# Two running sums of a depthwise convolution: from SBUF tiles to two PSUM banks

## The chip, the core and the metric

The kernel runs on one core of one Trainium2 chip. The metric is device time in microseconds (us) of one execution; lower is better. Five engines work side by side, each through its own queue in order: TensorE (PE, matmuls, with its weight loads as PEld), VectorE (DVE), ScalarE (ACT), GpSimd (POOL) and SyncE (SP, which here only issues DMAs). SBUF is the on-chip memory for operands, PSUM the memory of eight banks into which PE writes.

## What is computed

A trunk of four layers over 512 image tokens and 256 context tokens of width 1024: attention, neighbourhood attention, a convolution module, a Fourier mixer, each followed by an MLP of width 4096. The change is in the third mixer, which works on the image tokens alone:

```python
def conv_module(h, w_pw1, b_pw1, w_dw, b_dw, ln_g, ln_b, w_pw2, b_pw2):
    a, g = jnp.split(h @ w_pw1 + b_pw1, 2, axis=-1)
    u = a * jax.nn.sigmoid(g)
    pad = CONV_WIDTH // 2            # CONV_WIDTH = 31
    u = lax.conv_general_dilated(u, w_dw[:, None, :], window_strides=(1,), padding=[(pad, pad)],
                                 dimension_numbers=('NWC', 'WIO', 'NWC'),
                                 feature_group_count=u.shape[-1]) + b_dw
    u = jax.nn.silu(layer_norm(u, ln_g, ln_b))
    return u @ w_pw2 + b_pw2
```

For each feature the convolution is a sum of 31 products: tap t of that feature times the token sequence moved by t.

## The kernel before

Features lie on partitions, 128 at a time, so the 1024 features are eight blocks j = 0 to 7, each a tile of 128 partitions by 512 tokens. Matmuls take their operands as two parts (high and low, made by `split`, lines 101 to 104), and `mm3` (lines 119 to 126) makes three matmuls of each product: lines 123, 124 and 126.

The convolution layer is `l2` (line 909). Its main loop runs over the eight blocks. For a block it loads and splits two weight tiles (ACT makes the high part `wh`, POOL the low part `wl` for j > 0), lets PE make the two halves of the first projection in `ps_mm` (48 matmuls), and calls `conv_input` (line 1087 on): ACT takes the sigmoid (L1091), DVE makes `u` from PSUM (L1095), ACT rounds it to `uH` (L1100), DVE makes the rest `uL` (L1102). Then the taps of the block follow, in `conv_taps` (line 1104), for blocks 0 to 6:

- The first 9 taps (10 in blocks 5 and 6, `PE_TAPS`) go to PE as diagonal matrices `dg`, which ACT makes in pairs (L1112, L1113, four buffers each); their sum, with a mean that is taken off (L1116), comes about in `ps_cv`.
- The other 22 (21) taps are DVE's. `acc` holds two sums, `y` and a temporary `tmp_t`, both in SBUF. The first two taps start the sums (L1122, L1124); each further one is a scalar_tensor_tensor, acc = u * w + acc, alternating between the sums (L1126, 138 in all). Then DVE adds the two sums (L1128) and PE's part (L1130).

The finished `y` is summed up with its square for the layer norm: ACT squares it (L943), POOL adds both (L941, L944). Block 7 has no taps on DVE: ACT and POOL make all its 31 diagonals beforehand (L953, L954, five after each block), and PE makes its taps for half the tokens at a time (L960, L963, L964). Behind the first half and 36 matmuls of the second stands the column sum of the statistics (L981), which needs all sums, and with it the layer norm of the first half of the tokens begins.

Order: DVE's instructions in this stage are kept in program order (`keep`), as are the diagonals of block 7. `advance` interleaves them: the taps of block j - 1 on DVE run while PE makes the projection of block j, and `u` of block j stands among them. All else is ordered by a scheduler that simulates the program. PSUM in this layer has four banks for `mm`, two for `cv` and two for `st`; `st` is used by the statistics before and behind the taps, and by nothing during them.

Of the kernel before, what the change touches and what calls it, by code (L numbers as in the profile page):

```python
# [10 lines left out]
R = mybir.dt.float32r  # L11
# [5 lines left out]
P = 128  # L17
# [10 lines left out]
TAPS = 31  # L28
# [5 lines left out]
# columns of the vector table  # L34
# [14 lines left out]
class Trunk:  # L49
# [10 lines left out]
    # ---------------------------------------------------------------- pools  # L60
# [14 lines left out]
    def psum(self, pool="psum", **roles):  # L75
        """PSUM tiles by role: name = (banks of a tile, tiles)."""
        if pool in self.pools:
            self.close(pool)
        p = self.open(pool, space=bass.MemoryType.PSUM)
        for r, (banks, bufs) in roles.items():  # L80
            self.roles[r] = p, banks, bufs
# [14 lines left out]
    # ---------------------------------------------------------------- pieces  # L96
    def load(self, dst, src):
        """a load that none traced later overtakes"""
        self.last_load = self.tc.keep_in_program_order(self.nc.sync.dma_start(dst, src)).ins

    def split(self, src, H, L, low=None):
        """H + L = src, both with float32r's 12 significant bits."""
# [3 lines left out]
    def weight(self, src, pool=None, n=P, bufs=None, raw_bufs=None, low=None):  # L106
        """A block of 1024 rows and n columns, split: [P, KC, n] twice."""
# [11 lines left out]
    def mm3(self, outs, lhs, rhs, k, last):  # L119
        """outs[i] += (lH + lL)^T (rH + rL), without the product of the two low parts."""  # L120
# [7 lines left out]
    def rstd(self, ss, n, role="n"):  # L128
        """(ss / n + eps) ** -0.5, with a Newton step behind the square root's table"""
# [11 lines left out]
    def bcast(self, cols, nb):  # L141
        """[tokens, 1] columns -> every partition holds all tokens (in PSUM)."""
# [15 lines left out]
    def part(self, t, c0, c1):  # L158
        """a part of the tokens: c0:c1, or the image rows that make up c0:c1 of the natural order"""
# [4 lines left out]
    def like(self, t):  # L164
        """a compact tile of such a part"""
# [5 lines left out]
    def modulate(self, j, c0, c1, Rp, gs, sh, hj):  # L171
        """hj <- split(x_j * R * g * (1 + scale) + shift)"""
# [8 lines left out]
    def stat(self, j, c0, c1, S, add=None):  # L181
        """S += x_j^2"""
# [25 lines left out]
    # ---------------------------------------------------------------- ada_ln  # L208
# [15 lines left out]
    def ada_dots(self, t, vs, cols):  # L224
        """The second of two vectors goes to GpSimd and ScalarE, in place."""
# [12 lines left out]
    def ada_finish(self, layer, g, vs):  # L238
        """Bias of chunk group g, and the products that the norms and the biased layers want."""
# [34 lines left out]
    def load_sb(self, nv):  # L274
        """silu of the conditioning vectors, in every partition."""
# [4 lines left out]
    # ---------------------------------------------------------------- phases  # L280
# [25 lines left out]
    def mod_tile(self, l, nv):  # L306
        """The six modulation vectors of layer l as columns, and the products made of them."""
# [10 lines left out]
    def start(self):  # L318
# [8 lines left out]
        # silu of the conditioning vectors, as columns and in every partition  # L327
# [22 lines left out]
        # modulation, norm and the products for k and v advance together over the features  # L350
# [30 lines left out]
        def shift(i):  # L381
            """the shift of half the features, as rows, then as columns"""
# [35 lines left out]
    # ------------------------------------------------------ layer 0: attention  # L418
# [41 lines left out]
    def qk_unit(self, ps, tp, a, g, wk, tab, qkg):  # L460
        """rms norm, rope, split and transpose of 256 tokens x 4 heads (a: 0 q, 1 k)."""
# [58 lines left out]
    def recip_rows(self, sums, w, wk, rp):  # L520
        """1 / sums [P queries, blocks, 2 heads] -> rows [(head, feature), query]"""
# [12 lines left out]
    def fold(self, pv, hh, t):  # L534
        """t's rows of head hh <- the sum of the products with V's high and low parts"""
# [4 lines left out]
    def scale_pv(self, t, rb, dst):  # L540
        """dst <- split(t * rb)"""
# [4 lines left out]
    def l0b(self):  # L546
# [11 lines left out]
        # 256 latent queries, then 256 more, then the context's own, which see the context only  # L558
# [6 lines left out]
        def front(pair, part, hh, u):  # L565
            """the probabilities of 128 queries, transposed and split"""
# [26 lines left out]
        def back(pair, part, hh, half):  # L593
            """half of the keys: both parts of V, side by side, against the split probabilities"""
# [31 lines left out]
        # output projection  # L626
# [17 lines left out]
    # ---------------------------------------------------------------- linear  # L644
    def proj_part(self, wtiles, acts, c0, c1, md, gate, gs, sh, md_next, h_next, rate=0, role="mm", early=0):
        """x += gate * (W^T acts) for the tokens c0:c1, then their norm into h_next."""
# [26 lines left out]
    def mlp(self, layer, T, next_h):  # L673
        """next_h(): opens the tiles that the norm after this block fills."""
# [60 lines left out]
    def swap_h(self, T, name):  # L735
        """Replaces the dead tiles of h by new ones on the same side."""
# [6 lines left out]
    # -------------------------------------------- layer 1: neighbourhood attention  # L743
    def l1a(self):
        """q, k, v of all heads, split, into scratch memory."""
# [7 lines left out]
        # bias and mask of a head: zeros for the context, then the three cases of the window  # L753
# [13 lines left out]
        # v keys: context chunks, then latent chunks that start 8 columns before a block  # L767
# [41 lines left out]
    def l1b(self):  # L809
# [29 lines left out]
        def front(head, b):  # L839
            """the probabilities of 128 queries, transposed and split"""  # L840
# [18 lines left out]
        def back(head, part):  # L859
            """a quarter of a head's products with v"""  # L860
# [6 lines left out]
            # context chunks serve all queries; latent chunk j serves the blocks j - 1 and j  # L867
            for vc in ((0,), (1,), (3, 4), (5, 2))[part]:
                for s in range(2):
# [6 lines left out]
                    elif j > 0:  # L876
                        # second half of the window of block j - 1, first half of that of block j
# [33 lines left out]
    # -------------------------------------------- layer 2: convolution module  # L911
    def l2(self):
# [9 lines left out]
        # the mean of the first 128 features is taken off all of them before the statistics  # L922
# [23 lines left out]
        # all taps of the last features go to the tensor engine, for half of the tokens at a time  # L946
# [375 lines left out]
```

## Time and profile before

| | |
|---|---|
| timed runs | 2802.20, 2808.11 and 2809.17 us, median 2808.11 |
| span of the profiled execution | 2802.3 us; no other time of it is listed, and the fastest timed run is 0.1 us shorter |
| busy over the span | PE 95%, DVE 66%, ACT 42%, POOL 16% |
| stage of the taps on DVE | from 1743 to 1904 us of the span |

The busy shares are means over the whole trunk, in which stages with different limits follow each other. How long an engine was busy in a stage, and what it or the next engine waited for, is read in the stage's own window. An instruction's duration can overlap the next one's start on the same engine, so the pace of a row of instructions is the difference of their starts.

### The profile page before, as it was taken

To read this page: it belongs to the slowest core of one execution; us is meant where nothing else is said; L and a number is where in the kernel's file an instruction comes from. 1 tells how busy PE (TensorE), PEld (TensorE's weight loads), DVE (VectorE), ACT (ScalarE), POOL (GpSimd) and SP (SyncE) were. 2 spreads that over 40 slices of the span, in tenths; PEclk is the share of its full clock that TensorE was granted. 3 is DMA by queue.
4 is the path that set the end of the run, shared out by engine and by line. 5 is a ranking of instruction groups with operands and counts; after the bars stand their busy time and mean duration, and the time that the engine had idled before them with its cause. 6 is when DMAs were issued, how large, how long until landed. Compare 5 with 4: busy or idle time off the path is not lost.

```text
span 2802.3 us, 39962 instructions
## 1 busy us (share of the span) xinstructions
PE 2648.6 (95%) x15452; PEld 2329.9 (83%) x15452; DVE 1841.1 (66%) x2868; ACT 1169.6 (42%) x2087; POOL 460.6 (16%) x373
## 2 busy tenths in 40 slices
PE   5978989999999999999999999888999998999998
PEld 3967878888888888988988889668888887988888
DVE  8897989766453372268766657998766657744435
ACT  4438884312121352278522336444422335533323
POOL 4251122000000040034200005452100003200002
PEclk9989999999999999999999999989999999999999
DMA  7251135344443257488466634112466643333334
GB/s 265 66 169 38 35 125 188 107 149 140 151 139 98 68 161 215 135 202 209 153 207 206 200 117 142 46 53 68 142 200 201 202 127 128 122 105 98 95 95 126
DMA packets 124557, 384.86 MB, mean 137 GB/s; under 512 B 17232, under 2 KB 37840, under 8 KB 123088
## 3 DMA queue, kind: packets, MB, share of 16 engines
q1 hardware_dynamic: 121104, 379.16, 43.5%
q10 hardware_dynamic: 3264, 3.15, 0.3%
q8 instruction: 122, 2.00, 0.3%
q14 instruction: 67, 0.55, 0.1%
HBM read 354.98 MB, written 27.26 MB: 136 GB/s over the span
## 4 chain that ended last, share of the span: by engine, by line
PE 45%; DVE 8%; ACT 1%; DMA 1%; issue 1%; POOL 1%; DVEq 0%; ACTq 0%; POOLq 0%; SPq 0%
PE ps_mm L123 14%; PE ps_mm L126 14%; PE ps_mm L124 14%; DVE y L1126 2%; DVE tmp_t L1126 2%; DMA k<-k 1%; DVE wl L104 1%; DVE h L179 0%; PE ps_s L846 0%; PE ps_pt L855 0%; PE ps_cv L960 0%; PE ps_cv L963 0%; DVE cv L1042 0%; PE ps_cv L964 0%; DVE u L1095 0%
## 5 line engine op out<-in xcount | busy, mean ns | idle before, releaser
L103 ACT CAST wh<-raw 128x1024 fp32r<-128x1024 f32 (+1 forms) x397 | 419.6, 1060 | 1030.6 <-PE ps_mm L124 609.4
L104 DVE TENSOR_TENSOR wl<-raw,wh 128x1024 fp32r<-128x1024 f32 (+1 forms) x368 | 464.8, 1265 | 372.9 <-ACT wh L103 370.1
L191 POOL TENSOR_TENSOR S<-S,tmp_q 128x256 f32<-128x256 f32 (+1 forms) x104 | 145.4, 1398 | 1680.1 <-ACT tmp_q L190 1677.7
L123 PE MATMUL ps_mm<-u,wh 128*128 128x512 f32 (+1 forms) x1088 | 374.9, 346 | 0.0
L124 PE MATMUL ps_mm<-u,wh 128*128 128x512 f32 (+1 forms) x1088 | 373.8, 345 | 0.0
L126 PE MATMUL ps_mm<-u,wl 128*128 128x512 f32 (+1 forms) x1088 | 373.6, 346 | 0.0
L124 PE MATMUL ps_mm<-hm,wh 128*128 128x512 f32 (+1 forms) x912 | 331.0, 365 | 0.0
L126 PE MATMUL ps_mm<-hm,wl 128*128 128x512 f32 (+1 forms) x912 | 330.8, 365 | 0.0
L123 PE MATMUL ps_mm<-hm,wh 128*128 128x512 f32 (+1 forms) x912 | 328.1, 366 | 1.5 <-ACT hm L178 1.1
L203 DVE SCALAR_TENSOR_TENSOR x<-ps_mm,mod,x 128x256 f32<-128x256 f32 (+1 forms) x192 | 114.8, 602 | 247.3 <-PE ps_mm L126 247.3
L220 DVE CUSTOM_DVE_ANT_0 prod<-araw,sb 128x1024 bf16<-128x1024 f32 x216 | 272.7, 1262 | 1.4 <-DMA araw<-in_ada 0.5
L124 PEld LDWEIGHTS ps_mm<-u,wh 128*128 128x128 f32 x1088 | 206.1, 189 | 25.1
L123 PEld LDWEIGHTS ps_mm<-u,wh 128*128 128x128 f32 x1088 | 205.7, 189 | 25.4 <-DVE x L203 0.4
L126 PEld LDWEIGHTS ps_mm<-u,wl 128*128 128x128 f32 x1088 | 205.8, 189 | 25.0
L126 PEld LDWEIGHTS ps_mm<-hm,wl 128*128 128x128 f32 x912 | 172.4, 189 | 27.5 <-DVE wl L104 0.4
L124 PEld LDWEIGHTS ps_mm<-hm,wh 128*128 128x128 f32 x912 | 172.5, 189 | 27.3
L123 PEld LDWEIGHTS ps_mm<-hm,wh 128*128 128x128 f32 x912 | 170.7, 190 | 29.2 <-ACT hm L178 1.5
L103 ACT CAST u<-tmp_r 128x512 fp32r<-128x512 f32 (+2 forms) x143 | 89.1, 624 | 170.7 <-DVE tmp_r L703 170.5
L123 PE MATMUL ps_big<-hm,wh 128*128 128x512 f32 x464 | 157.4, 339 | 0.8 <-ACT wh L103 0.8
L104 DVE TENSOR_TENSOR u<-tmp_r,u 128x512 fp32r<-128x512 f32 (+2 forms) x143 | 99.0, 695 | 86.5 <-ACT u L103 86.2
L124 PE MATMUL ps_big<-hm,wh 128*128 128x512 f32 x464 | 145.9, 337 | 0.0
L123 PE MATMUL ps_mm<-wh,h 128*128 128x256 f32 x448 | 131.3, 294 | 10.2 <-ACT h L178 6.6
(317 smaller groups left out, 5956.1 us busy)
## 6 DMA issues: line engine op xcount, KB each, us to landing
raw<-in_w SPq DMA_DIRECT2D x288, 512.0 KB, 3.9
araw<-in_ada SPq DMA_DIRECT2D x176, 512.0 KB, 3.7
raw<-in_wo SPq DMA_DIRECT2D x32, 512.0 KB, 4.0
raw<-in_wpw SPq DMA_DIRECT2D x24, 512.0 KB, 3.6
raw<-in_wqk SPq DMA_DIRECT2D x16, 512.0 KB, 4.1
q<-q SPq DMA_DIRECT2D x32, 256.0 KB, 8.1
raw<-in_wft SPq DMA_DIRECT2D x16, 512.0 KB, 3.8
k<-k SPq DMA_DIRECT2D x32, 224.0 KB, 8.4
```

The lines of the kernel that those rows point to most:

```text
L103: self.nc.scalar.copy(out=H, in_=src)
L104: (low or self.nc.vector).tensor_tensor(out=L, in0=src, in1=H.bitcast(F), op=ALU.subtract)
L123: mm(o, lhs[0], rh, start=(k == 0), stop=False)
L124: mm(o, lhs[0], rl, start=False, stop=False)
L126: mm(o, lhs[1], rh, start=False, stop=last)
L191: (add or nc.gpsimd).tensor_tensor(out=S[:, :w], in0=S[:, :w], in1=q, op=ALU.add)
L203: self.nc.vector.scalar_tensor_tensor(out=xm, in0=self.like(ps), scalar=gate[:, m:m + 1], in1=xm, op0=ALU.mult, op1=ALU.add)
L220: ins = self.nc.vector.tensor_tensor_reduce(out=junk, in0=t, in1=self.sb[:, v], op0=ALU.mult, op1=ALU.add, scale=1.0, scalar=0.0, accum_ou ...
L1126: keep(nc.vector.scalar_tensor_tensor(out=a, in0=ut, scalar=wt, in1=a, op0=ALU.mult, op1=ALU.add))
```

## The change

`acc` becomes two PSUM tiles of the role `st` in place of `y` and `tmp_t`. The last tap of the first sum writes `y` in SBUF, and the addition of the two sums takes its first input from PSUM. The number of instructions on every engine stays.

```diff
-        acc = (y, self.tmp("t"))
+        acc = [self.ps("st") for _ in range(2)]
...
             else:
-                keep(nc.vector.scalar_tensor_tensor(out=a, in0=ut, scalar=wt, in1=a, op0=ALU.mult, op1=ALU.add))
+                last = t >= TAPS - 2 and a is acc[0]
+                keep(nc.vector.scalar_tensor_tensor(out=y if last else a, in0=ut, scalar=wt, in1=a, op0=ALU.mult, op1=ALU.add))
             yield
-        keep(nc.vector.tensor_tensor(out=y, in0=y, in1=acc[1], op=ALU.add))
+        keep(nc.vector.tensor_tensor(out=y, in0=acc[1], in1=y, op=ALU.add))
```

(The full diff also drops comments, which moves line numbers by one: L1126, L1128 and L1130 of before are L1127, L1129 and L1131 now.)

DVE, from the last taps of block 0 to the first of block 1, before (the names ahead of the arrow are written, those behind it read; the numbers on `y` tell the tiles of blocks apart):

```order
L1126 SCALAR_TENSOR_TENSOR y_16663<-u,vecs,y_16663 128x512
L1126 SCALAR_TENSOR_TENSOR tmp_t<-u,vecs,tmp_t 128x512
L1128 TENSOR_TENSOR y_16663<-y_16663,tmp_t 128x512
L1130 TENSOR_TENSOR y_16663<-ps_cv,y_16663 128x512
L1122 TENSOR_SCALAR y_16664<-u,vecs 128x512
L1124 TENSOR_SCALAR tmp_t<-u,vecs 128x512
L1126 SCALAR_TENSOR_TENSOR y_16664<-u,vecs,y_16664 128x512
```

Here each tap reads two tiles in SBUF, `u` and the sum (`vecs` holds the tap's weight, one number for each partition), and writes SBUF. The same place on DVE in the changed kernel:

```order
L1127 SCALAR_TENSOR_TENSOR y_16663<-u,vecs,ps_st 128x512
L1127 SCALAR_TENSOR_TENSOR ps_st<-u,vecs,ps_st 128x512
L1129 TENSOR_TENSOR y_16663<-ps_st,y_16663 128x512
L1131 TENSOR_TENSOR y_16663<-ps_cv,y_16663 128x512
L1122 TENSOR_SCALAR ps_st<-u,vecs 128x512
L1124 TENSOR_SCALAR ps_st<-u,vecs 128x512
L1127 SCALAR_TENSOR_TENSOR ps_st<-u,vecs,ps_st 128x512 x10
```

Nothing moved on DVE; the sums did, so that each of these reads one tile in SBUF at most, and all but three of a block write PSUM.

The scheduler's order of the other engines shifts a little with it. ACT around the square of block 2's `y` (L943), before (`dg` are PE's diagonals of the next taps, `wh` a weight tile's high part, `tmp_q` the sigmoid):

```order
L943 ACTIVATE tmp_r<-y_16665 128x512
L953 ACTIVATE dg_16673<-ident,wdH 128x128 x5
L103 CAST wh<-raw 128x1024
L1091 ACTIVATE tmp_q<-ps_mm,vecs 128x512
L1112 ACTIVATE dg_17424<-ident,wdH 128x128
L1113 ACTIVATE dg_17425<-ident,wdL 128x128
```

And in the changed kernel:

```order
L103 CAST wh<-raw 128x1024
L1091 ACTIVATE tmp_q<-ps_mm,vecs 128x512
L1112 ACTIVATE dg_17427<-ident,wdH 128x128
L1113 ACTIVATE dg_17428<-ident,wdL 128x128
L1112 ACTIVATE dg_17434<-ident,wdH 128x128
L1113 ACTIVATE dg_17435<-ident,wdL 128x128
L943 ACTIVATE tmp_r<-y_16665 128x512
```

The weight tile, the sigmoid and two pairs of diagonals moved ahead of the square, which waits for DVE's L1131. The order in which PE mixes taps and projection shifts by a few matmuls in the same way, and POOL takes some weight tiles before a sum instead of behind it.

## Rows read from the trace of the kernel before

**Rows 1.** Chain of waits, 1743 to 1904 us: shares by engine, tile, line.

```profile
by line: DVE y L1126 34.2%; DVE tmp_t L1126 27.1%; DVE tmp_t L1124 4.1%; DVE u L1095 3.8%; DVE y L1128 3.5%; DVE y L1130 2.6%; DVE uL L1102 2.5%; DVE y L1122 2.5%; PE ps_cv L960 2.5%; PE ps_cv L963 2.4%; PE ps_cv L964 2.3%; issue 1.7%; POOL
```

**Rows 2.** Windows, block 2: length, PE, PEld, DVE, ACT, POOL, clock, DMA, GB/s.

```profile
1812.00:1836.00 24.00, 19.13 (x72) 15.19 (x71) 23.86 (x27) 11.54 (x30) 12.55 (x11) 0.86 0.21 66
```

**Rows 3.** Waits, 1743 to 1903 us: total us, times, longest.

```profile
ACT uH L1100 <- DVE u L1095: 37.2, 6, 8.6
...
PE ps_cv L123 <- ACT dg L1112: 17.2, 6, 4.9
```

**Rows 4.** Timeline of DVE and POOL: start us, duration us, instruction.

```profile
1769.50 0.74 DVE L1126 SCALAR_TENSOR_TENSOR tmp_t<-u,vecs,tmp_t 128x512 f32<-128x512 f32 x1
1769.90 2.62 POOL L104 TENSOR_TENSOR wl<-raw,wh 128x1024 fp32r<-128x1024 f32 x1 [4.40 <-ACT wh L103]
1770.16 2.90 DVE L1126 SCALAR_TENSOR_TENSOR y<-u,vecs,y 128x512 f32<-128x512 f32 x1
1772.98 0.74 DVE L1126 SCALAR_TENSOR_TENSOR tmp_t<-u,vecs,tmp_t 128x512 f32<-128x512 f32 x1
```

**Rows 5.** DVE's groups, 1743 to 1904 us: count, busy us, mean ns, idle before.

```profile
L1126 DVE SCALAR_TENSOR_TENSOR y<-u,vecs,y 128x512 f32<-128x512 f32 x70 | 73.1, 1044 | 0.0
L1126 DVE SCALAR_TENSOR_TENSOR tmp_t<-u,vecs,tmp_t 128x512 f32<-128x512 f32 x68 | 59.1, 869 | 0.0
L1128 DVE TENSOR_TENSOR y<-y,tmp_t 128x512 f32<-128x512 f32 x7 | 9.0, 1287 | 0.2
L1124 DVE TENSOR_SCALAR tmp_t<-u,vecs 128x512 f32<-128x512 f32 x7 | 8.5, 1220 | 0.0
...
L1122 DVE TENSOR_SCALAR y<-u,vecs 128x512 f32<-128x512 f32 x7 | 5.1, 724 | 0.0
```

**Rows 6.** Timeline of POOL and DVE in the layer norm behind the taps.

```profile
1932.31 2.42 POOL L104 TENSOR_TENSOR wl<-raw,wh 128x1024 fp32r<-128x1024 f32 x1 [5.55 <-ACT wh L103]
...
1932.43 0.41 DVE L1031 TENSOR_TENSOR y<-y,ps_st 128x256 f32<-128x256 f32 x1
1932.76 0.47 DVE L1033 SCALAR_TENSOR_TENSOR y<-y,vecs,ps_st 128x256 f32<-128x256 f32 x1
1933.15 1.85 DVE L1042 TENSOR_TENSOR cv<-v,cv 128x256 fp32r<-128x256 f32 x1
```

**Rows 7.** Timeline of DVE: u and uL among taps, a block's start and end.

```profile
1754.84 1.14 DVE L1095 SCALAR_TENSOR_TENSOR u<-ps_mm,vecs,tmp_q 128x512 f32<-128x512 f32 x1
...
1757.75 0.74 DVE L1126 SCALAR_TENSOR_TENSOR y<-u,vecs,y 128x512 f32<-128x512 f32 x1
...
1766.66 0.54 DVE L1122 TENSOR_SCALAR y<-u,vecs 128x512 f32<-128x512 f32 x1
1767.11 0.48 DVE L1124 TENSOR_SCALAR tmp_t<-u,vecs 128x512 f32<-128x512 f32 x1
...
1786.61 0.74 DVE L1126 SCALAR_TENSOR_TENSOR tmp_t<-u,vecs,tmp_t 128x512 f32<-128x512 f32 x1
1787.38 0.69 DVE L1128 TENSOR_TENSOR y<-y,tmp_t 128x512 f32<-128x512 f32 x1
1788.17 0.69 DVE L1130 TENSOR_TENSOR y<-ps_cv,y 128x512 f32<-128x512 f32 x1
1788.78 0.54 DVE L1122 TENSOR_SCALAR y<-u,vecs 128x512 f32<-128x512 f32 x1
```

**Rows 8.** Timeline of PE, and the column sum from the chain of waits.

```profile
1736.62 0.40 PE L124 MATMUL ps_mm<-h,wh 128*128 128x512 f32 x1
...
1740.28 0.39 PE L126 MATMUL ps_mm<-h,wl 128*128 128x512 f32 x1
...
1897.00 0.28 PE L960 MATMUL ps_cv<-uH,dg 128*128 128x256 f32 x1
1897.12 0.28 PE L963 MATMUL ps_cv<-uL,dg 128*128 128x256 f32 x1
...
1908.33 0.79 PE ps_st L981 x8
```

## The prediction

> **What bounds the kernel now.** I read the chain of waits first, cut to the stage that the diff touches. Between 1743 and 1904 us it is DVE's: the taps of L1126 alone are 34.2% and 27.1% of it, PE appears with the taps of block 7 at the stage's end only [rows 1]. The window of one block agrees: in 24.0 us DVE is busy for 23.86 and PE for 19.13, with PE's clock granted at 0.86 of full speed [rows 2]. Then the waits: ACT stood 37.2 us in six pieces at L1100 for DVE's `u`, and PE 17.2 us in six pieces for the diagonals that stand behind L1100 in ACT's queue [rows 3]. So PE is late because DVE is late, and a microsecond of DVE in this stage is worth nearly a microsecond of the kernel, until PE has no idle time left to give.
>
> Why is DVE late? The timeline of DVE beside that of POOL shows it. An undisturbed tap takes 0.74 us, and the next one starts 0.66 us after it. POOL begins a weight tile's low part at 1769.90, which takes 2.62 us; the tap that DVE begins at 1770.16 takes 2.90 us, and the one after it 0.74 again [rows 4]. The stretched tap ends when POOL's instruction has ended. Over the stage: 138 taps were busy for 73.1 + 59.1 = 132.2 us; 138 x 0.74 is 102.1, so 30.1 us are stretching. L1128 has 9.0 us for 7 where an undisturbed one takes 0.69: 4.2 more. L1124 has 8.5 where 7 x 0.48 is 3.4: 5.1 more. L1122 has 5.1 where 7 x 0.54 is 3.8: 1.3 more [rows 5, 7]. Together **40.7 us**, a quarter of the stage.
>
> **The change part by part.**
>
> *What goes.* The stretching is tied to what DVE reads. In the layer norm, POOL's weight tile runs from 1932.31 to 1934.73. Within it DVE does L1031 and L1033, whose second input is in PSUM, in 0.41 and 0.47 us, starting 0.33 and 0.39 apart; the very next instruction, L1042, reads two tiles in SBUF and takes 1.85 us, until POOL is done [rows 6]. After the change, the taps, L1122, L1124 and L1129 read one tile in SBUF. I take all of the 40.7 us away from them. What can still be stretched is `uL` (L1102, two SBUF inputs, 7 times): POOL was busy for 12.55 of 24 us [rows 2], and a stretched instruction lost up to 2.90 - 0.74 = 2.2 us [rows 4]; half of seven at half of that is some 4 us, between 0 and 15; I take 3.
>
> *What a tap costs then.* No row shows DVE writing PSUM. Bounds from below: L1130, which reads PSUM and adds, has a pace of 0.61 us (1788.17 to 1788.78) [rows 7]. From above: if each tap waited for the one before to land, as L1128 waits for the last tap, 0.77 us (1786.61 to 1787.38) [rows 7]. Reading PSUM costs a scalar_tensor_tensor nothing to be seen: L1033 on 256 elements has a pace of 0.39, and the 0.66 of a tap in SBUF on 512 is that plus 256 elements at about 1.05 ns each (0.27). I take **0.66 us**, unchanged, as that row is the nearest to the new instruction.
>
> [...]
>
> L1122 and L1124 start the sums with one tile and constants, at 0.54 and 0.48 us and a pace of 0.45 for L1122 (1766.66 to 1767.11) [rows 7]. With PSUM as output they may fall to the rate of L1130. I take 0.61 for both; at worst 14 x 0.16 = 2.2 us against staying at 0.45.
>
> *DVE's sum.* Taps 138 x 0.66 = 91.1, and 7 x 0.11 for the wait of L1129 on the last one, 0.8; the starts 14 x 0.61 = 8.5; L1129 7 x 0.79 (1787.38 to 1788.17) = 5.5; L1131 and the one L1139, 8 x 0.61 = 4.9; `u` and `uL` 7 x 1.59, which is 1757.75 - 1754.84 less two taps [rows 7], 11.1. That is 121.9, with the 3 us for `uL` **125 us**, so that DVE would be through at 1868 instead of 1904.
>
> *What is late next: PE.* From 1736.62 to 1740.28 are 16 matmuls of 512 columns, 0.229 us each at full clock [rows 8]. By that pace 28 of block 1's 48 are done at 1743; 20 are left, 6 x 48 for blocks 2 to 7, 65 x 3 for the taps of blocks 0 to 6, and 7 for the means: 510, or 116.8 us. Ahead of the column sum L981 then stand block 7's first half, 93 of 256 columns, one for the mean, and 36 of the second half: 130 at 0.12 (1897.00 to 1897.12) = 15.6 us [rows 8]. Together **132.4 us**: L981 cannot come before 1875.4, where it came at 1908.33 [rows 8]. So PE caps the gain at 32.9 us, whatever DVE does. Behind DVE's last row two sums on POOL and two on DVE follow, while PE does its 36; they end close to PE, and I put no extra on them. The cap holds only if PE never waits. Of its 17.2 us of waiting for diagonals [rows 3] I keep 3: DVE's period of a block (125 / 7 = 17.9 us) is hardly above PE's (76 x 0.229 = 17.4), so either waits for the other now and then. In the changed order ACT makes some diagonals ahead of the square of `y`, which eases that. With PE nearly always at work I count its clock as full, as in the rows used.
>
> L981 then comes at 1878.4, **29.9 us** earlier. Nothing behind it is touched: the same matmuls follow, and the chain goes on with PE. I let the whole 29.9 through.
>
> *Costs at nothing.* The two PSUM banks were idle during the taps; the statistics take them only after L1131 of block 6. The order among the sums is as before, each tap waiting for the tap two ahead of it, which is done after 0.74 us while its successor starts 1.32 us later. POOL's own work would hide at 12.6 of 18 us, ACT's at 11.5 [rows 2]; if DVE's cover of 24 us were kept, they would cost nothing at all, and without it they still fit.
>
> **The rivals.**
>
> *Writes to PSUM land late.* Each tap at 0.77 us, the upper bound. DVE's sum is then 121.9 + 138 x 0.11 + 3 = 140, L981 comes some 5 us behind DVE's end, as it does today (1904 to 1908.33) [rows 8], at about 1743 + 140 + 5 = 1888, and the gain is 20 us: 2788. Against it: L1033 and L1130 show no such delay on reads.
>
> *The stretching stays.* POOL may hold DVE for another reason than the second tile, for instance for `u` itself, read from SBUF by every tap. Then only the 2 us of L1122 and L1124 come on top: 2808 to 2811. Against it: L1033 also reads `y` from SBUF, inside POOL's instruction, and was not held [rows 6].
>
> *Slower: the sum is read and written in the same bank.* A tap reads an element of a bank and writes one to it at the same time. If the bank gave DVE only one of the two at a time, the elements' part of a tap, 2 x 0.27 = 0.54 us from the paces above, would double. 138 x 0.54 = 74 us more make DVE's 125 into 199; L981 would come at 1743 + 199 + 5 = 1947, 39 us later: 2847. It decides from a pace of 0.66 + 35 / 138 = 0.91 us on. In the rows nothing speaks for it but that no instruction of DVE's reads and writes one bank.
>
> **How the numbers follow.** The profiled execution spans 2802.3 us; less 29.9 it is 2772.4. The median of the runs lies 5.8 above that span, so I forecast **2778 us**. Chances: forecast 0.80 (2768 to 2785, from the full cap on the fastest runs to the page's price and a few more microseconds of waiting); late writes 0.10 (2785 to 2795); stretching stays 0.05; one bank 0.05. The range takes in the first two: 2768 to 2794. About 0.3% (8 us) is what a measurement of this kernel can tell from no change: faster 0.90, same 0.05, slower 0.05.
>
> **What would show it.** In the changed profile the taps' durations should have no tail near 2.9 us, and their mean should be close to their median; if it is the median that moved to 0.85 or more, writes land late, and above 1.1 it is the bank. DVE's share of a block's window should fall below full, PE's rise to full with the clock at 1.0, and the chain of waits in the stage should be PE's for the larger part. L981 should start near 1878; if DVE ends near 1868 but L981 stays behind 1885, the gain went into PE waiting for ACT's diagonals. Stretched taps beside POOL's weight tiles would refute the whole.

## The result, and the profile of the changed kernel

| | before | after |
|---|---|---|
| timed, median (range, runs) | 2807.93 us (2802.20 to 2809.17, 4) | 2771.04 us (2768.41 to 2774.47, 4) |
| ratio, 95% interval | 1 | 0.9872 (0.9857 to 0.9887) |
| span of the profiled execution | 2802.3 us | 2769.1 us |
| first `u` (L1095) of the stage to the first column sum (L981) | 167.7 us | 134.1 us |
| busy over the span: PE, DVE, POOL | 2648.6, 1841.1, 460.6 us | 2633.1, 1807.7, 443.1 us |

The change made the kernel 36.9 us faster by the medians, 33.2 by the two spans; 2778 was forecast, with 2768 to 2794 as range.

The stage is taken here from the start of the first `u` to the start of the first product of the statistics, L981, since the work ahead of it comes up to 2.4 us earlier or later in profiles of one and the same code. Before, `u` and L981 start here (timeline of DVE and PE; start us, duration us, instruction; the 1908.33 of [rows 8] is L981 in the chain of waits, where it counts from the end of the matmul ahead of it):

```profile
1740.50 1.15 DVE L1095 SCALAR_TENSOR_TENSOR u<-ps_mm,vecs,tmp_q 128x512 f32<-128x512 f32 x1 [6.95 <-ACT tmp_q L1091]
...
1908.17 0.95 PE L981 MATMUL ps_st<-ones,S 128*128 128x1 f32 x8
```

After:

```profile
1742.86 1.15 DVE L1095 SCALAR_TENSOR_TENSOR u<-ps_mm,vecs,tmp_q 128x512 f32<-128x512 f32 x1 [6.95 <-ACT tmp_q L1091]
...
1876.91 0.95 PE L981 MATMUL ps_st<-ones,S 128*128 128x1 f32 x8
```

The stage went from 167.7 to 134.1 us, 33.6 us less, and what lies behind L981 from 894.1 to 892.1.

The same instructions as in [rows 5], by tile: count, then the shortest, median and longest duration in ns:

```profile
L1127 DVE SCALAR_TENSOR_TENSOR ps_st<-u,vecs,ps_st x131: 735/747/775, 1746.8 to 1869.7; 128x512 f32<-128x512 f32 x131
...
L1122 DVE TENSOR_SCALAR ps_st<-u,vecs x7: 806/806/809, 1745.4 to 1855.5; 128x512 f32<-128x512 f32 x7
L1124 DVE TENSOR_SCALAR ps_st<-u,vecs x7: 744/746/747, 1746.1 to 1856.2; 128x512 f32<-128x512 f32 x7
L1127 DVE SCALAR_TENSOR_TENSOR y<-u,vecs,ps_st x7: 733/735/751, 1760.3 to 1870.4; 128x512 f32<-128x512 f32 x7
L1129 DVE TENSOR_TENSOR y<-ps_st,y x7: 691/691/692, 1761.7 to 1871.1; 128x512 f32<-128x512 f32 x7
```

The tail is gone: the longest of 138 taps is 0.775 us, where the taps of [rows 5] had means of 1.044 and 0.869. POOL works beside them as before. One block on POOL and DVE, to be read against [rows 4]:

```profile
1784.78 2.41 POOL L104 TENSOR_TENSOR wl<-raw,wh 128x1024 fp32r<-128x1024 f32 x1
1787.15 1.29 POOL L944 TENSOR_TENSOR S<-S,tmp_r 128x512 f32<-128x512 f32 x1
1788.42 2.92 POOL L954 TENSOR_SCALAR dg<-ident,wdL 128x128 fp32r<-128x128 f32 x5
...
1784.65 6.67 DVE L1127 SCALAR_TENSOR_TENSOR ps_st<-u,vecs,ps_st 128x512 f32<-128x512 f32 x10
```

Ten taps in 6.67 us, beside three kinds of POOL's instructions, are a pace of (6.67 - 0.75) / 9 = 0.658 us. What is held now is `uL`, which reads two tiles in SBUF (by tile, as above). Three of its eight took 1.58 to 2.43 us; in the kernel before none of them was longer than 0.72.

```profile
L1102 DVE TENSOR_TENSOR uL<-u,uH x8: 708/738/2426, 1744.8 to 1859.9; 128x542 fp32r<-128x542 f32 x8
```

The windows of one block and of the whole stage (length, PE, PEld, DVE, ACT, POOL, clock, DMA, GB/s), against [rows 2]:

```profile
1745.42:1876.91 131.49, 130.18 (x627) 108.72 (x626) 127.98 (x184) 77.03 (x190) 62.32 (x58) 1.00 0.21 61
1783.00:1801.00 18.00, 18.00 (x79) 14.67 (x78) 17.86 (x27) 11.41 (x31) 11.06 (x12) 1.00 0.20 60
```

PE is busy all but 1.3 us, at a granted clock of 1.00 where it had been 0.86; DVE is nearly full as well. The whole stage before, from `u` to L981, shows that PE gained in two ways:

```profile
1740.50:1908.17 167.67, 145.03 (x639) 117.05 (x637) 162.26 (x185) 75.31 (x193) 80.45 (x59) 0.92 0.16 51
```

PE was idle for 22.6 us of it, and busy for 145.0 us, at a mean granted clock of 0.92, with what takes it 132.7 us now (1742.86 to 1876.91, clock 1.00). So 21.3 of the 33.6 us are waits of PE that went, and 12.3 go with the higher clock (by an estimate from these windows, 145.0 x 0.92 = 133.4). The waits of [rows 3] are down to this (engine, line waited for, total us, times, longest; the two of PE are at the taps of block 7, which need its `uL` and a bank that ACT reads out first):

```profile
ACT uH L1100 <- DVE u L1095: 3.5, 2, 3.0
...
PE ps_cv L963 <- DVE uL L1102: 0.8, 1, 0.8
...
PE ps_cv L960 <- ACT y L970: 0.6, 1, 0.6
```

But the chain of waits over 1745 to 1877 us still names DVE:

```profile
by line: DVE ps_st L1127 57.2%; DVE uL L1102 6.9%; DVE u L1095 5.7%; PE ps_cv L963 4.1%; PE ps_cv L960 4.0%; PE ps_cv L964 3.9%; DVE ps_st L1122 3.8%; DVE ps_st L1124 3.5%; DVE y L1129 3.2%; DVE y L1131 3.1%; DVE y L1127 3.0%; issue 0.9%; D
```

Of two engines that are both full, the chain shows one. Which of them sets the end now is what half of the experiments are about.

### The profile page after: what moved, and what is told of

It reads as the page before. It is cut to its first block, busy times and chain, and to the rows that moved or that the text cites. A ratio compares the mean times of both kernels' runs of the same rounds, so it can differ in the third digit from the quotient of the medians.

```text
span 2769.1 us, 39970 instructions
## 1 busy us (share of the span) xinstructions
PE 2633.1 (95%) x15452; PEld 2320.4 (84%) x15452; DVE 1807.7 (65%) x2868; ACT 1171.3 (42%) x2087; POOL 443.1 (16%) x373
## 4 chain that ended last, share of the span: by engine, by line
PE 44%; DVE 7%; ACT 1%; issue 0%; POOL 0%; DVEq 0%; ACTq 0%; POOLq 0%
PE ps_mm L123 14%; PE ps_mm L126 14%; PE ps_mm L124 14%; DVE ps_st L1127 3%; DVE wl L104 1%; DVE h L179 0%; DVE uL L1102 0%; DVE u L1095 0%; PE ps_cv L960 0%; PE ps_cv L963 0%; PE ps_cv L964 0%; DVE tmp_t L176 0%; DVE x L203 0%; POOL S L191 0%; DVE ps_st L1122 0%
## 5 line engine op out<-in xcount | busy, mean ns | idle before, releaser
L191 POOL TENSOR_TENSOR S<-S,tmp_q 128x256 f32<-128x256 f32 (+1 forms) x104 | 145.2, 1396 | 1679.7 <-ACT tmp_q L190 1675.7
```

Of the source, the lines that this page charges most:

```text
L191: (add or nc.gpsimd).tensor_tensor(out=S[:, :w], in0=S[:, :w], in1=q, op=ALU.add)
```

## The experiments

In all tables below, "stage" is from the first `u` to the first L981 and "behind" is from there to the end of the span, both in us of the profiled execution. The line numbers of some kernels are off by a few, as their edits add lines. Each ratio is to runs of the kernel before made beside that kernel, whose medians lie between 2803.61 and 2807.97 us, so small differences are better read from the ratios and the stages than from the times.

| kernel | timed, median us | ratio (95%) | stage | behind |
|---|---|---|---|---|
| before | 2807.93 | 1 | 167.7 | 894.1 |
| after | 2771.04 | 0.9872 (0.9857 to 0.9887) | 134.1 | 892.1 |
| after, again | 2768.58 | 0.9860 (0.9846 to 0.9875) | 134.0 | 891.7 |
| one sum in PSUM | 2794.37 | 0.9956 (0.9940 to 0.9971) | 155.7 | 895.6 |
| before, no weights on POOL | 2784.87 | 0.9920 (0.9905 to 0.9935) | 147.8 | 894.5 |
| after, no weights on POOL | 2774.28 | 0.9881 (0.9866 to 0.9896) | 134.7 | 895.7 |
| before, more work on POOL | 2814.72 | 1.0032 (1.0021 to 1.0043) | 175.2 | 895.8 |
| after, more work on POOL | 2772.47 | 0.9888 (0.9873 to 0.9903) | 134.0 | 892.0 |
| after, a tap less on PE | 2782.02 | 0.9919 (0.9905 to 0.9934) | 139.6 | 895.5 |
| after, a tap more on PE | 2773.93 | 0.9891 (0.9875 to 0.9908) | 137.0 | 894.0 |
| after, sums started by ACT | 2768.14 | 0.9861 (0.9845 to 0.9877) | 132.1 | 894.6 |
| the same, a tap less on PE | 2773.11 | 0.9878 (0.9862 to 0.9895) | 132.7 | 894.6 |
| after, `v` in PSUM | 2776.10 | 0.9899 (0.9884 to 0.9914) | 134.0 | 898.4 |
| after, half of `v` in PSUM | 2771.78 | 0.9876 (0.9860 to 0.9893) | 134.0 | 892.5 |

The changed kernel, run again beside the two kernels with ACT's starts, gave what was expected, and tells how far its own runs go: eight runs from 2767.16 to 2774.47 us.

> The changed kernel again, unchanged, beside the two others: 2768 to 2775 us, as the reference that their verdicts are read against.

### Is it the tile that DVE reads? One sum alone in PSUM

```diff
-        acc = (y, self.tmp("t"))
+        acc = (y, self.ps("st"))
...
-        keep(nc.vector.tensor_tensor(out=y, in0=y, in1=acc[1], op=ALU.add))
+        keep(nc.vector.tensor_tensor(out=y, in0=acc[1], in1=y, op=ALU.add))
```

> Only the second sum (tmp_t) lies in PSUM, the first stays in y in SBUF; the addition of both reads one of each. Theory (holding): a POOL instruction holds the first DVE instruction with two SBUF inputs that comes up while it runs, until it ends. Every second tap is still such a one, so a 2.4 us weight tile still catches a tap; where a PSUM tap comes first, 0.66 us of it are used. Of the 40.7 us the 21 on taps of y stay, some 6 of the 9 on the other taps reappear there, L1124 (5 us) and the addition (4 us) are free: gain about 12 us against before, 2796 (2791 to 2800), with taps on ps_st near 0.75 us each and those on y with a mean of about 1.1 us. Rival (each tap in PSUM saves its own share): half of the taps, half of the whole change's 37 us, 2789 or less, and the mean of the taps on y falls.

2794.37 us, within 2 us of the holding theory. The same instruction, at the same time, with the sum in one memory or the other (timeline of DVE and POOL):

```profile
1769.07 0.75 DVE L1126 SCALAR_TENSOR_TENSOR ps_st<-u,vecs,ps_st 128x512 f32<-128x512 f32 x1
1769.72 2.43 DVE L1126 SCALAR_TENSOR_TENSOR y<-u,vecs,y 128x512 f32<-128x512 f32 x1
1772.08 0.74 DVE L1126 SCALAR_TENSOR_TENSOR ps_st<-u,vecs,ps_st 128x512 f32<-128x512 f32 x1
...
1769.20 2.40 POOL L104 TENSOR_TENSOR wl<-raw,wh 128x1024 fp32r<-128x1024 f32 x1 [4.45 <-ACT wh L103]
```

And over the stage, by tile:

```profile
L1126 DVE SCALAR_TENSOR_TENSOR y<-u,vecs,y x70: 723/743/2899, 1744.7 to 1888.4; 128x512 f32<-128x512 f32 x70
...
L1126 DVE SCALAR_TENSOR_TENSOR ps_st<-u,vecs,ps_st x68: 741/744/751, 1745.3 to 1887.7; 128x512 f32<-128x512 f32 x68
```

Both kinds of tap alternate on one engine beside one POOL. Those with two tiles in SBUF take up to 2.90 us; of those with one, none is held. It is what the tap reads that counts: in the changed kernel the last tap of the first sum reads PSUM and writes SBUF, and none of these seven was held either (longest 0.751 us above), though three of them ran beside a weight tile on POOL. So `u` in SBUF does not hold a tap up, which refutes the rival in which the stretching stays. The held tap ends 0.55 us after POOL's instruction (1772.15 against 1771.60), the one of [rows 4] 0.54 us after it (1773.06 against 1772.52): most of a tap's pace of 0.66 us is still to come once POOL is through.

The two starts of a block are another case, which the account by the second tile does not cover. L1122 and L1124 read one tile in SBUF, `u`, before as after. Still, five of the seven L1124 of the kernel before took 1.49 to 1.52 us instead of 0.48, each beside an addition on POOL (timeline of DVE and POOL, before):

```profile
1789.23 1.52 DVE L1124 TENSOR_SCALAR tmp_t<-u,vecs 128x512 f32<-128x512 f32 x1
...
1789.01 1.47 POOL L941 TENSOR_TENSOR S<-S,y 128x512 f32<-128x512 f32 x1 [1.45 <-DVE y L1130]
```

With one sum in PSUM, L1122 still writes SBUF and L1124 writes PSUM (by tile):

```profile
L1122 DVE TENSOR_SCALAR y<-u,vecs x7: 539/542/1433, 1743.6 to 1873.4; 128x512 f32<-128x512 f32 x7
L1124 DVE TENSOR_SCALAR ps_st<-u,vecs x7: 741/748/750, 1744.0 to 1873.9; 128x512 f32<-128x512 f32 x7
```

L1124 stands beside the same additions of POOL and is not held any more (0.750 us at the longest); some of L1122 are, for up to 1.43 us: the seven took 5.6 us, where 7 x 0.54 is 3.8. So the start that writes PSUM was freed. Why one that reads a single tile and writes SBUF is held, no run here shows.

### Is POOL the cause? Weights' low parts taken off POOL, and work added to it

In the first two kernels the low parts of the first projection's weights no longer go through POOL: ACT writes those tiles as plain copies, and the subtraction is left out. Of POOL's 14 weight tiles in the stage, 4 are left.

```diff
-            W = [self.weight(io["wpw1"][2 * j + e], low=nc.gpsimd if j else None) for e in range(2)]
+            W = [self.weight(io["wpw1"][2 * j + e], low="act" if j else None) for e in range(2)]
```

> The kernel before, sums in SBUF, but the low parts of the projection's weight tiles for blocks 1 to 7 are made by ACT as a plain copy instead of by POOL as a difference (the difference is left out, so the products are not the right ones; the amount of PE work is the same). Theory (holding): without POOL's 14 weight tiles the taps of 2.8 us vanish, 24 us on taps and some 5 on L1128 and L1122; the milder stretching beside POOL's sums and diagonals (about 11 us) stays. Stage some 27 us shorter: 2780 (2774 to 2788), although nothing lies in PSUM. Rival (PSUM itself is what makes the taps quicker): no gain, 2804 to 2811.

> The same edit on the changed kernel (the difference is left out again). Theory: only uL can still be held, 3.7 us of DVE in all, and PE has no idle time left to give: 2767 to 2772. Rival (POOL's weight tiles cost time in another way, say by being late for PE): a gain as large as in e2, 2745 to 2755.

Before loses 20.4 us of its time by it (against 2805.23 in the same comparison) and 19.8 of its stage. DVE's groups in its stage (count, busy us, mean ns, idle), to be read against [rows 5]:

```profile
L1130 DVE SCALAR_TENSOR_TENSOR y<-u,vecs,y 128x512 f32<-128x512 f32 x70 | 59.2, 846 | 0.0
L1130 DVE SCALAR_TENSOR_TENSOR tmp_t<-u,vecs,tmp_t 128x512 f32<-128x512 f32 x68 | 58.9, 865 | 0.0
...
L1128 DVE TENSOR_SCALAR tmp_t<-u,vecs 128x512 f32<-128x512 f32 x7 | 8.6, 1227 | 0.0
...
L1132 DVE TENSOR_TENSOR y<-y,tmp_t 128x512 f32<-128x512 f32 x7 | 4.8, 692 | 0.2
```

Of the 40.7 us of stretching, 59.2 + 58.9 - 102.1 = 16.0 are left in the taps and 5.2 in the start of the second sum, 21.2 in all; 19.5 went, and the stage became 19.8 us shorter. What is left goes with the work that POOL still has: diagonals, sums, four weight tiles. It missed the expectation by 5 us above the single number, inside its range. The changed kernel, with the same work taken off POOL, gained nothing (2774.28, 2 us above the expected range): its stage grew by 0.7. DVE now waited 3.2 us for `uH` of the busier ACT, but PE's waits stayed at 1.4, so what the 0.7 went into stays open. Ten weight tiles on POOL were thus worth 20 us of the stage before, and are worth nothing after.

The other way round, two additions of 128x512 were added on POOL for each block, 14 in all, onto a tile that nobody waits for, before and after.

```diff
             diagonals(5 * j, 5 * j + 5)
+            for _ in range(2 if j else 0):
+                nc.gpsimd.tensor_tensor(out=junk, in0=h[0][:, 0].bitcast(F), in1=h[0][:, 1].bitcast(F), op=ALU.add)
```

> The kernel before with two more POOL additions of 128x512 behind the diagonals of each of blocks 1 to 7, 14 in all at about 1.3 us, on tiles that nobody waits for. POOL has the time (12.6 of 24 us busy in a block). Theory (holding): each holds a tap for about 1.0 us, as the sums do in before (1.78 instead of 0.74): 14 us slower, 2822 (2816 to 2828). Rival (no holding): POOL's idle time takes it, 2804 to 2811.

> The changed kernel with the same 14 extra POOL additions as e4. Theory (holding): taps read one SBUF tile and are not held; only uL can meet one of them, at most 1 us each, and POOL has 8 us of a block free: 2769 to 2775. Rival (POOL slows DVE whatever it reads): 14 us slower, 2785.

Before: 2814.72 us, slower by 0.32%, or 9.5 us by the medians measured side by side (2805.23 before), where 14 were expected; 2814.72 is just below the expected range. The timeline of POOL, then of DVE, tells why:

```profile
1728.39 8.59 POOL L1017 TENSOR_TENSOR junk<-h 128x512 f32<-128x512 f32 x6
...
1753.44 6.87 POOL L1017 TENSOR_TENSOR junk<-h 128x512 f32<-128x512 f32 x4
...
1753.95 1.80 DVE L1129 SCALAR_TENSOR_TENSOR y<-u,vecs,y 128x512 f32<-128x512 f32 x1
1755.68 1.80 DVE L1129 SCALAR_TENSOR_TENSOR tmp_t<-u,vecs,tmp_t 128x512 f32<-128x512 f32 x1
1757.40 1.79 DVE L1129 SCALAR_TENSOR_TENSOR y<-u,vecs,y 128x512 f32<-128x512 f32 x1
1759.11 1.75 DVE L1129 SCALAR_TENSOR_TENSOR tmp_t<-u,vecs,tmp_t 128x512 f32<-128x512 f32 x1
```

Nothing waits for the additions, so the scheduler put six of them ahead of the stage, where no tap runs. Eight lay beside DVE, and four of these in a row held four taps in a row by 1.0 to 1.1 us each: 1.75 to 1.80 instead of 0.74, and not 2.90, since an addition of 512 elements is shorter on POOL (1.31 us at its shortest here) than a weight tile of 1024 (2.40). The stage grew by 7.5 us (167.7 to 175.2), 0.9 for each of the eight; here a tap is held for longer where POOL's instruction is longer. After: ten taps lie at 6.67 us and two at 1.41 beside the same additions; one `uL` beside them took 1.60, and the stage is 134.0 as without them. The 2785 us of the rival did not come.

### What sets the stage's end now? Taps moved between PE and DVE

PE does the first 9 or 10 taps of a block by diagonals, DVE the others. One tap of each of seven blocks was moved to DVE, and in a second kernel one to PE.

```diff
-PE_TAPS = (9,) * 5 + (10,) * 2
+PE_TAPS = (8,) * 5 + (9,) * 2
```

```diff
-PE_TAPS = (9,) * 5 + (10,) * 2
+PE_TAPS = (10,) * 5 + (11,) * 2
```

> The changed kernel with one tap of each of blocks 0 to 6 moved from PE to DVE (PE_TAPS 8 and 9). DVE gets 7 x 0.66 = 4.6 us more, PE 21 matmuls or 4.8 us less. In the changed trace DVE's chain to the column sum ends within 1 us of PE's. Theory (both are at their limit): DVE decides, 4 us slower, 2775 (2773 to 2778). Rival (PE alone is the limit, and DVE has room): 4 to 5 us faster, 2766.

> The changed kernel with one tap of each block moved from DVE to PE (PE_TAPS 10 and 11). Theory (both at their limit): PE decides, 21 matmuls at 0.2275 us, 4 to 5 us slower, 2776 (2773 to 2779). Rival (DVE alone is the limit): 4 to 5 us faster, 2766.

Both are slower than the changed kernel, by some 12 and 4 us (against 2769.9, the median of its eight runs), or by some 15 and 7 by the ratios. With a tap more the time lies inside the expected range; with a tap less it lies 4 us above it. With a tap more, PE is the limit alone. The window of its stage (columns as above):

```profile
1741.47:1878.46 136.99, 136.99 (x660) 114.71 (x659) 120.22 (x178) 84.25 (x207) 63.88 (x59) 1.00 0.21 62
```

PE is busy for all of it, DVE for 120.2. The stage is 2.9 us longer than in the changed kernel. With a tap less, DVE is late and PE runs dry near the end. Its timeline of PE, and the windows around that place:

```profile
1845.77 0.40 PE L1116 MATMUL ps_cv<-y0H,neg 128*128 128x512 f32 x1
1849.85 0.49 PE L123 MATMUL ps_cv<-uH,dg 128*128 128x512 f32 x1 [3.68 <-ACT uH L1100]
...
1855.41 0.63 PE L126 MATMUL ps_cv<-uH,dg 128*128 128x512 f32 x1
1855.84 0.63 PE L123 MATMUL ps_cv<-uH,dg 128*128 128x512 f32 x1
...
1850.00:1857.00 7.00, 6.36 (x15) 4.79 (x16) 6.89 (x11) 3.22 (x9) 0.00 (x0) 0.52 0.17 63
1857.00:1861.00 4.00, 3.30 (x14) 2.29 (x13) 3.97 (x6) 1.79 (x5) 3.12 (x3) 0.99 0.01 2
```

PE stood for 3.68 us, since `uH` comes from `u`, which DVE makes in its turn among the taps. Behind that the granted clock was 0.52 for 7 us, and a matmul of 512 columns took 0.43 us from start to start (1855.41 to 1855.84) instead of 0.23: some 3.4 us more. PE was spared 4.8 us, waits grew from 1.4 to 7.0 us in all, the clock took 3.4 here and some 1.7 more behind two shorter gaps later (from 1864.04 to 1867.24 us matmuls of 256 columns start 0.21 us apart instead of 0.12; the mean clock from 1860 to 1880 is 0.91): the stage is 5.6 us longer. Another 3.3 us lie behind L981, where PE's waits are 2.3 us longer in all; the rest is open, and the profiled run is the fastest of four. That it would be slower, and by DVE, was expected; the second price of a gap, its clock, was not.

### Both limits at once: the sums started by ACT

DVE's time is cut without a change of PE's: ACT writes the first product of each sum into PSUM.

```diff
-                keep(nc.vector.tensor_scalar(out=a, in0=ut, scalar1=wt, scalar2=self.vec("b_dw")[:, j:j + 1], op0=ALU.mult, op1=ALU.add))
+                nc.scalar.activation(a, ut, AF.Identity, scale=wt, bias=self.vec("b_dw")[:, j:j + 1])
...
-                keep(nc.vector.tensor_scalar(out=a, in0=ut, scalar1=wt, scalar2=None, op0=ALU.mult))
+                nc.scalar.activation(a, ut, AF.Copy, scale=wt)
```

> The changed kernel, with ScalarE instead of VectorE writing the first product of each of the two running sums into PSUM (7 blocks x 2 starts). Theory (at 131.5 us the stage is bound by TensorE, whose 640 matmuls fill 130.3 us of it, and VectorE's 127.2 us only lie close beside): VectorE loses 14 starts (7 x 0.71 + 7 x 0.65 = 9.5 us) and nothing comes of it but the last us in which VectorE's tail ends together with TensorE: 2770 to 2772 us, the statistics' first product some 131 us behind the stage's start. Rival (VectorE alone sets the stage's end, as the chain of waits reads, 55% of which lies in the taps): 9.5 us of it go, 2762 to 2765 us.

2768.14 us, against 2768.58 of the changed kernel in the same comparison: no difference that can be measured, although DVE lost 14 instructions of 9.6 us by their paces. The time lies between the two expected ranges, 1.9 us below that of the theory and 3.1 above the rival's; the stage decides between them. Its stage, and the chain of waits over it:

```profile
1738.02:1870.10 132.08, 132.08 (x639) 110.78 (x638) 115.73 (x171) 87.49 (x207) 64.02 (x59) 1.00 0.21 65
...
by line: PE ps_mm L126 17.3%; PE ps_mm L123 17.1%; PE ps_mm L124 17.1%; PE ps_cv L126 11.8%; PE ps_cv L124 11.8%; PE ps_cv L123 11.8%; PE ps_cv L960 4.0%; PE ps_cv L964 3.9%; PE ps_cv L963 3.9%; PE ps_cv L1116 1.1%; PE ps_cv L1136 0.2%; PE 
```

Now PE never waits, and the chain is PE's from end to end. PE's own work in the stage is thus 132.1 us (the kernel with a tap more, where PE never waits either, agrees: 137.0 less 4.8 for 21 matmuls), and the changed kernel's 134.1 lie 2.0 above it, 1.4 of which are the two waits shown ahead. Those 2 us are all that a faster DVE can gain. Here they were gained, and 2.5 us more were spent behind L981: PE's waits there are 1.4 us longer in all, the rest is open.

Then with a tap less on PE besides:

> The same, and one tap of each of seven blocks moved from TensorE to VectorE (8 or 9 on TensorE in place of 9 or 10). Theory of two engines with little room on either: TensorE loses 21 matmuls of 512 columns (4.8 us at 0.229), VectorE gains 7 taps (4.6 us at 0.658) and loses the starts (9.5 us), so that both end earlier: stage 126 to 128 us instead of 131.5, 2765 to 2768 us; without ScalarE's starts the same shift of taps made it 2782, with TensorE idle for 3.7 us and at the low clock behind that. Rival (TensorE runs dry as it did there, because the split of u, not the starts, comes too late): 2775 or more.

2773.11 us: slower than the changed kernel beside it, outside both expected ranges but nearer to the rival's 2775. PE waits, and the window behind that:

```profile
PE ps_cv L960 <- ACT uH L1100: 1.9, 1, 1.9
...
1858.00:1860.00 2.00, 2.00 (x12) 2.00 (x11) 2.00 (x4) 0.00 (x0) 0.00 (x0) 0.50 0.00 0
```

By the changed kernel's measure, its two waits included, the stage would be 134.1 - 4.8 = 129.3 us; 1.9 us of new waiting and some 1.7 us at the low clock (0.72, 0.50 and 0.93 in three windows of 2 us) make it 132.9, and it was 132.7. The gain on PE was real, and PE's own gap took most of it back; 2.5 us more are behind L981 again. Against the kernel with ACT's starts alone (132.1) nothing was gained.

### The layer norm's held instruction: is there more to get?

Behind the taps L1042 was held in [rows 6]. Its input `v` was put into PSUM, into the two banks of the role `cv`.

```diff
-            t = wk.tile([P, 256], F, tag="v", name="v", bufs=3)
+            t = self.ps("cv")[:, :256]
```

> The changed kernel with the same step at another place: in the layer norm behind the taps the tile v, from which ACT makes the high and DVE (L1042) the low part, lies in PSUM (role cv, two banks) instead of SBUF (three buffers). Theory (holding): L1042 reads one SBUF tile, its stretched ones (1.8 to 2.1 us instead of 0.42, four on the chain in before) vanish: 4 us faster, 2767 (2764 to 2770). Rival (two banks instead of three buffers make DVE wait for ACT): no gain or 1 to 3 us slower, 2771 to 2774.

2776.10 us, slower than the changed kernel and above both expected ranges. By tile, the held instruction, which is not held any more, and the one that writes `v` and still reads two tiles in SBUF; then one of PE's waits behind 1876 us (L152 is the column sum of the next norm, L191 the sum that it needs):

```profile
L1042 DVE TENSOR_TENSOR cv<-ps_cv,cv x16: 408/411/418, 1885.3 to 1927.7; 128x256 fp32r<-128x256 f32 x16
...
L1038 DVE SCALAR_TENSOR_TENSOR ps_cv<-y,vecs,sg x16: 473/490/2425, 1884.1 to 1926.8; 128x256 f32<-128x256 f32 x16
...
PE ps_st L152 <- POOL S L191: 10.0, 1, 10.0
```

The hold moved on to L1038, up to 2.43 us where the changed kernel has 1.15, and a wait of 10.0 us stands where the changed kernel has 0.3. My reading was that the second half's products, which use the `cv` banks too, could not begin before DVE's last `v` had left them: they start at 1927.62, with DVE's last L1038 at 1926.76, and at 1914.22 in the changed kernel. The last kernel puts that to the test: only the first half's `v` in PSUM.

```diff
-            t = wk.tile([P, 256], F, tag="v", name="v", bufs=3)
+            t = wk.tile([P, 256], F, tag="v", name="v", bufs=3) if c0 else self.ps("cv")[:, :256]
```

> The changed kernel, with the layer norm's tile v in a PSUM bank of the role cv for the first half of the tokens alone; the second half's v stays in SBUF, as in the changed kernel. With all of v in PSUM the time behind the statistics grew by 6 us (898.3 us from L981 to the end instead of 892.2), and TensorE waited 10.0 us. Theory (the two cv banks were the cause: the second half's products need them, and VectorE's last v of the second half gave them free only then): with the second half back in SBUF that wait goes, and the time is that of the changed kernel or a little less, 2766 to 2771 us, since L1042 of the first half is no longer held. Rival (L1038, which reads two tiles in SBUF, is now held in L1042's place, and that hold moved the order of the work behind it): 2774 or more, as with all of v in PSUM.

2771.78 us, a little above the expected range. The second half's products start at 1911.81, the wait is down to 1.5 us, the part behind L981 to 892.5, as in the changed kernel; and L1038 of the first half is still held, for up to 2.43 us:

```profile
L1038 DVE SCALAR_TENSOR_TENSOR ps_cv<-y,vecs,sg x8: 470/489/2433, 1884.0 to 1908.3; 128x256 f32<-128x256 f32 x8
...
PE ps_st L152 <- POOL S L191: 1.5, 1, 1.5
```

So the banks were the cause of the 6 us, and taking one held instruction away gained nothing, because the next one with two tiles in SBUF was held in its place. No kernel tried was measurably faster than the changed one.

## Why the prediction was right, and where its sizes were off

**The mechanism** held for the taps and for the addition of the two sums, 34.3 of the 40.7 us. Their stretching goes with the second tile in SBUF: one kernel shows both kinds side by side (up to 2.899 us with two tiles there, 0.751 with one), two show that it is worth POOL's work (19.8 us of stage for the 19.5 that went with ten weight tiles), and two that it grows with that work before and no longer does after. The two held taps set beside POOL's instruction end 0.54 and 0.55 us behind it; by what the one holds up the other, no run here shows.

**The starts** were right by luck. The prediction took their 6.4 us away too, on the ground that L1122 and L1124 read one tile in SBUF after the change. They did so before it as well, and were held (up to 1.85 and 1.52 us), so by that reason nothing would have changed. They were freed as they write PSUM now (0.81 and 0.75 us at the longest), as the kernel with one sum there shows for L1124.

**A tap in PSUM** at 0.66 us, taken from the row nearest to it: measured 0.658. Neither late writes (0.77) nor a bank that serves one access at a time (1.20) showed. The taps all in SBUF had 0.66 too, and L1130 of before, which reads PSUM, had 0.61 [rows 7]. The chance of 0.80 takes times up to 2785 in, and counts a price for taps on PSUM among them; no run shows such a price, and in its place stands the pace of 0.658 us.

**DVE's sum** was 125 us and is 127.2 (1745.42 to the end of L1131 at 1872.63). The starts have paces of 0.71 and 0.65 us, not 0.61 (7 x 0.14 = 1.0 more); `u` and `uL` take 15.1 us together and not 14.1, with three of the `uL` held; the rest agrees to 0.2. It cost 2.0 us of the stage at most, as PE was the limit.

**PE's cap** decided the result, and was the step that was mis-sized. I counted 510 matmuls of 512 columns in the stage; 497 are there in the trace (two of them under way at its start), before as after: 295 of the projection where I had 308, 195 of taps, 7 means. Block 1's projection had begun at 1730.92 already, mixed into that of block 0, and not at 1736.62. One of the three groups of the projection, after (count, busy us, mean ns):

```profile
L126 PE MATMUL ps_mm<-h,wl 128*128 128x512 f32 x99 | 38.6, 390 | 0.0
```

That is 13 x 0.23 = 3.0 us less. Their pace is 0.230 to 0.231 and not 0.229, 0.7 more. Of the waits for diagonals, for which I kept 3 us, 1.4 are there, and none for a diagonal. 135.4 - 3.0 + 0.7 - 1.6 = 131.5, which is what the windows show. So the stage became 33.6 us shorter instead of 29.9 (the sum gives 33.8; the rest is the chain's 1908.33 against the timeline's 1908.17). That none of PE's waits for diagonals is left goes with DVE's pace; ACT's order had shifted too, and no run separates the two.

**Behind L981** I expected nothing and got 2.0 us (2.4 in the second profile). Other kernels of this study show 891.7 to 895.8 there for the same code, so this is within what profiles differ by.

**From span to run** I added 5.8 us, the distance of the median from the one span. A run is only 1.9 us longer than its span (2770.98 for 2769.1); the other 3.9 were the place of that profiled execution among the runs of before. This was the largest error: 2802.3 - 29.9 + 1.9 would have been 2774.3. With the 3.7 us of the stage and the 2.0 behind it, less 2.4 by which the first `u` came later in this profile, it makes up the distance from 2778 to 2771.

**The chain of waits**, which I expected to be PE's for the larger part, names DVE with 57%. That expectation was wrong as a test: DVE's tail and PE end within 1 us of each other, and the chain follows one of them. The kernel in which ACT starts the sums decides for PE, and shows that a faster DVE is worth 2 us at most; that with a tap less on PE, where PE waits 7.0 us, shows that DVE has hardly any room either.

**The clock** at 1.00 in the stage, DVE's share just short of full, no tail near 2.9 us: as predicted.

## What to carry to other kernels

Where VectorE and GpSimd work side by side, look in the timeline for instructions of VectorE that end just behind one of GpSimd's, and count their inputs in SBUF: with one of two in PSUM the taps here were not held (0.775 us at the longest instead of 2.90), at the same pace (0.658 us). Instructions with a single input in SBUF were held as well: of the starts, L1124 took 1.49 to 1.52 us instead of 0.48, and 0.75 once it wrote PSUM. The gain ended here where the next engine was full (PE, busy for 132.7 of 134.1 us), so count that engine's instructions in the stage from its rows before believing a sum of saved time; and where two engines are full, move work between them only with a look at the waits, since a gap on TensorE cost a second time here by its clock (0.52 for 7 us behind a gap of 3.68 us). The two banks that took `v` held up the products that needed them next (they started at 1927.62 us instead of 1914.22; with half of `v` there, at 1911.81): see who needs a bank next.

## What the runs showed of the hardware

POOL became faster too, without an edit to it. Its weight tiles before and after, each by tile in the stage (shortest, median and longest in ns):

```profile
L104 POOL TENSOR_TENSOR wl<-raw,wh x14: 2409/2610/5369, 1744.9 to 1885.3; 128x1024 fp32r<-128x1024 f32 x14
```

```profile
L104 POOL TENSOR_TENSOR wl<-raw,wh x15: 2397/2407/2415, 1742.3 to 1853.4; 128x1024 fp32r<-128x1024 f32 x15
```

The stretching showed on both engines: POOL's busy time over the span fell from 460.6 to 443.1 us, and in the stage its weight tiles now lie within 18 ns of each other. I had not expected the delays of DVE to have such a counterpart.

A gap on PE of 0.75 us (and a later one of 0.56) left its clock at 1.00 in the changed kernel's stage. With ACT's starts and a tap less on PE, gaps of 1.9 and, behind one matmul, 0.8 us were followed by 0.50 in a window of 2 us, and in the kernel with a tap less alone one of 3.7 us by 0.52 in a window of 7 us.

A DVE instruction that starts a sum (one tile and constants) was slower when it wrote PSUM: a pace of 0.71 and 0.65 us where it was 0.45 and 0.40 in SBUF when nothing held it. The taps, which read a second tile, lost nothing (0.658 us, 0.66 in SBUF).
